# Gate logits of a hybrid encoder: pairs of tiles by seven block products, tanh through DRAM, gated sums on GpSimd

## Chip, cores, metric

The kernel runs on one core of a Trainium2 chip. The metric is the device time of one execution in microseconds (us), as the median of several runs. Engines are named as in the profile: PE (TensorE matmuls), PEld (its weight loads), DVE (VectorE), ACT (ScalarE), POOL (GpSimd), SP (SyncE, which here only issues DMAs).

## Reference

One layer of an encoder on x of 1024 positions by 1024 channels, in float32.

```python
h = rms_norm(x, g_mix[l])
z = h @ w_in[l]
u_fn, q, k, v, u_ssm, gate_logits = jnp.split(z, splits, axis=-1)
gates = jax.nn.sigmoid(gate_logits.reshape(b, s, N_BRANCH, D_MODEL))
y_fn = fourier_mix(u_fn) @ w_br_fn[l]
y_na = neighbourhood_attention(q * q_scale, k, v, na_rpb[l]) @ w_br_na[l]
y_ssm = ssm_branch(u_ssm, ...) @ w_br_ssm[l]
merged = gates[:, :, 0] * y_fn + gates[:, :, 1] * y_na + gates[:, :, 2] * y_ssm
x = x + merged @ w_out[l]
h = rms_norm(x, g_ffn[l])
x = x + jnp.square(jax.nn.relu(h @ w_up[l])) @ w_down[l]
```

The change concerns `gate_logits` (three times 1024 columns of `w_in`), the gates and the sum `merged`.

## The kernel before

All work is transposed: the normalised activations stand as `hT`, 1024 channels on 8 blocks of 128 partitions by 1024 positions in two halves of 512. Each float32 matmul is made of three on the fast float32 form: an operand is split in a high part (a cast on ACT) and a low part (a subtraction on DVE), and `three` multiplies high by high, high by low and low by high. So a weight tile of 128 output channels (128x1024, split as `wh` and `wl`) times `hT` for one half of the positions is 8 k-blocks x 3 = 24 matmuls of 128x512 (`proj`, line 171).

The middle of the kernel is a string of steps that sets the order in which work is written down. `q` steps make query and key, `t` steps (`logits`) make a tile of gate logits early and store its tanh in DRAM (`t_scr`), `fn` makes the Fourier input, `u` steps load a branch's rows from DRAM (`b_scr`, where they were spilled; the tiles are `act`), `at` finishes the attention, and `g` steps (`gate`) multiply a tile of a branch by its weight, form (tanh + 1) x product (line 1031, or 1029 for the first branch) and add it into the accumulator `mg` (line 1032). The first digit of `t` and `g` is the branch: 0 is the state space model (`ssm`), 1 the attention (`na`), 2 Fourier (`fn`); the second is the tile of 128 output channels, 0 to 7. In `gate`, tiles without an early `t` step make their logits in place: two halves of 24 matmuls. These are all 8 tiles of branch 0 and all 8 of branch 2. The last branch's sums are split into `mh` and `ml` (lines 199 and 200) for the output projection.

Three long computations (`ssm`, attention, Fourier) run as side generators: each third matmul of the main line calls `tick`, which lets a generator go on by its rate in steps. The order on each engine that results is fixed when the kernel is built; each engine works through its own list in order and waits at an instruction until its inputs and its buffers are there. SP's list of DMAs is such a list as well. Buffers come from pools: 36 slots of 4 KB per partition (`s`), 21 of 2 KB (`m`), 4 raw weights (`w`), 8 banks of PSUM.

Of the kernel before, what the change touches and what calls it, by code (L numbers as in the profile page):

```python
# [10 lines left out]
F32 = mybir.dt.float32  # L11
F32R = mybir.dt.float32r
I32 = mybir.dt.int32
AF = mybir.ActivationFunctionType
ALU = mybir.AluOpType

P = 128
# [3 lines left out]
H2 = 512  # L21
# [18 lines left out]
class Side:  # L40
    def __init__(self, gen, rate):
        self.gen = gen
        self.rate = rate
        self.credit = 0.0
        self.done = False
# [19 lines left out]
class Trunk:  # L65
# [806 lines left out]
    def queue(self):  # L872

        a = self.a
        wi = lambda i: (a["w_in"][i], [P, 8, P])
        q = [wi(14), wi(15)]
        q += [(a["w_v"][i], [P, 2, H2]) for i in range(4)]
        for step in self.steps:
            if step[0] == "q":
                q += [wi(2 + int(step[1])), wi(6 + int(step[1]))]  # L880
            elif step == "fn":
                q += [wi(0), wi(1)]
            elif step[0] in "tg":
                bi, d = int(step[1]), int(step[2])
                nm, br, kt, _ = self.order[bi]
                if step[0] == "t" or (bi, d) not in self.early:
                    q += [wi(16 + 8 * br + d)]
                if step[0] == "t":
                    self.early.add((bi, d))
                else:  # L890
                    q += [(a["w_br_" + nm][d], [P, kt, P])]
        q += [(a["w_out"][0, i], [P, 2, H2]) for i in range(4)]
        q += [(a["w_out"][1, i // 2][:, i % 2:i % 2 + 1, :], [P, 1, H2]) for i in range(8)]
        self.wq = q

    def run(self):
        nc, V, A, G = self.nc, self.nc.vector, self.nc.scalar, self.nc.gpsimd
        self.order = (("ssm", 2, 2, 0), ("na", 1, 4, 2), ("fn", 0, 2, 6))


        self.steps = ("t10 t11 q0 t12 q1 t13 t14 q2 t15 q3 t16 t17 fn u0 g00 g01 g02 at g03 g04 g05 g06 g07 u1 "
                      "g10 g11 g12 g13 g14 g15 u2 g16 g17 g20 g21 g22 g23 g24 g25 g26 g27").split()
        self.early = set()
        self.queue()
        self.zf, self.spilled = [], set()
# [15 lines left out]
        hT = []  # L921
# [4 lines left out]
        for half in range(2):  # L926
# [11 lines left out]
            for i in range(2):  # L938
                ps = self.proj(ws[i], hT, half)
# [9 lines left out]
        for t in range(8):  # L949
            half, c0 = t // 4, (t % 4) * P  # L950
            ps = self.ps([P, H2])
# [8 lines left out]
            r = 2 * (t % 2)  # L960
# [40 lines left out]
        acc = [None] * 8  # L1001
# [3 lines left out]
        def gate(bi, d):  # L1005
            nm, br, kt, ct = self.order[bi]
            act = acts[bi]
            early = (bi, d) in self.early
            if early:
                wb, = self.w_next(1, 1, 2)  # L1010
            else:
                wg, wb = self.w_next(2, 2, 2)
            if bi == 0:
                acc[d] = self.s([P, N], F32, "mg")
            for half in range(2):
                sl = slice(half * H2, half * H2 + H2)
                tg = self.m([P, H2], F32, "tg")
                if early:
                    self.dma(tg, self.t_scr[bi, d][:, sl])
                else:  # L1020
                    ps = self.proj(wg, hT, half)
                    A.activation(tg, ps, AF.Tanh, scale=0.5)  # L1022
                pb = self.ps([P, H2])
                pairs = []
                for k in range(kt):
                    pairs += self.three(wb[0][:, k, :], wb[1][:, k, :], *act[k][half])
                self.mm_main(pb, pairs)
                if bi == 0:
                    V.scalar_tensor_tensor(out=acc[d][:, sl], in0=tg, scalar=1.0, in1=pb, op0=ALU.add, op1=ALU.mult)
                    continue  # L1030
                V.scalar_tensor_tensor(out=tg, in0=tg, scalar=1.0, in1=pb, op0=ALU.add, op1=ALU.mult)
                V.tensor_tensor(out=acc[d][:, sl], in0=acc[d][:, sl], in1=tg, op=ALU.add)
                if bi == 2:
                    for q in (2 * half, 2 * half + 1):
                        if d % 4 == 0:
                            mg[q][d // 4] = (self.s([P, 4, 256], F32R, "mh"), self.s([P, 4, 256], F32R, "ml"))
                        hi, lo = mg[q][d // 4]
                        self.split(hi[:, d % 4, :], lo[:, d % 4, :], acc[d][:, 256 * q:256 * q + 256], 0.5)
            if bi == 2:
                acc[d] = None  # L1040

        def logits(bi, d):
            wg, = self.w_next(1, 1, 2)
            for half in range(2):
                ps = self.proj(wg, hT, half)
                tg = self.m([P, H2], F32, "tg")
                A.activation(tg, ps, AF.Tanh, scale=0.5)
                self.dma(self.t_scr[bi, d][:, half * H2:half * H2 + H2], tg)

        at, fft = None, None  # L1050
        need = (lambda: ssm, lambda: at, lambda: fft)

        def fetch(bi):
            need[bi]().finish()
            acts[bi] = self.unspill(self.order[bi][3], self.order[bi][2])

        for step in self.steps:
            if step[0] == "q":
                qk_in(int(step[1]))
                if at is None:  # L1060
                    at = self.side(attention(), 0.57)
            elif step == "fn":
                fn_in()
                fft = self.side(self.fft(), 0.5)
            elif step[0] == "u":
                fetch(int(step[1]))
            elif step == "at":
                at.finish()
            elif step[0] == "t":
                logits(int(step[1]), int(step[2]))  # L1070
            else:
                bi, d = int(step[1]), int(step[2])
                gate(bi, d)
                if d == 7:
                    acts.pop(bi)
# [5 lines left out]
        raw = [[None] * 8, [None] * 8]  # L1081
# [21 lines left out]
        for c in range(2):  # L1103
            wo = self.w_next(4 + 4 * c, 8 if c == 0 else 0, 8 if c == 0 else 1)
            cs = slice(c * H2, c * H2 + H2)
            for t in range(8):
                xr = self.m([P, H2], F32, "xr")
                self.dma(xr, self.a["x"][t * P:(t + 1) * P, cs])
                ps = self.ps([P, H2])
# [60 lines left out]
                t1[:] = []  # L1170

        ff.run()


class FeedForward:
# [8 lines left out]
    AHEAD_SUMS = 9  # L1184
    AHEAD_DOWN = 5
    RAW_DOWN = 9
    FIRST = 3
# [248 lines left out]
    def upto(self, name, steps, i, ahead, what):  # L1436
        at = self.done.get(name, 0)
        for s in steps[at:i + ahead + 1]:
            what(*s)
        self.done[name] = max(at, min(len(steps), i + ahead + 1))  # L1440

    def begin(self):

        n, first = self.PAIRS, range(self.FIRST)
        up = [(c, j) for j in (1, 2, 5, 6, 3, 7) for c in first]
        for c in range(self.FIRST, n):
            up.append((c, 1))
# [177 lines left out]
```

## Time and profile before

| what | value |
|---|---|
| time, median of 3 runs (lowest to highest) | 1411.34 us (1409.93 to 1414.94) |
| profiled execution, its own time | 1411.24 us |
| its span in the profile | 1409.5 us |
| mean granted clock of PE | 0.997 |
| PE busy, share of the span | 98% |
| DVE busy, share of the span | 67% |

The span is the time from the first to the last instruction in the profile; the rest of the profiled execution's time lies around it. An engine's busy time is the union of its instructions; matmuls overlap in it, so a matmul's own duration is longer than the distance from one start to the next.

### The profile page before, as it was taken

The page shows a single profiled execution, that of the slowest core. Times are in us where ns is not written, and L with a number is a line of the kernel's source. Part 1 is how long each engine was busy: PE and PEld are TensorE (multiplying, and loading weights), DVE is VectorE, ACT ScalarE, POOL GpSimd, SP SyncE. Part 2 cuts the span into 40 slices and gives each one's busy share as a digit, 9 for nine tenths or more (in the row PEclk, how much of TensorE's full clock was granted, in tenths as well). Part 3 has the DMA queues.
Part 4 walks back from the last instruction along what each step waited for, and adds up shares of the span by engine and source line. Part 5 has one row for each costly group of instructions (what it writes and reads, how often), then busy time and mean ns, then how long its engine had stood idle before and what let it go on. Part 6 is the DMA issues. An engine that isn't in the chain of part 4 may idle for free.

```text
span 1409.5 us, 18536 instructions
## 1 busy us (share of the span) xinstructions
PE 1376.9 (98%) x6520; PEld 1149.2 (82%) x6520; DVE 948.3 (67%) x1802; ACT 587.8 (42%) x1126; POOL 166.6 (12%) x345
## 2 busy tenths in 40 slices
PE   6999999999999999999999999999999999999997
PEld 5788878888888888888788788888888788888886
DVE  6778788768462314443516897777776899878767
ACT  5523454766552211122403664233333564444345
POOL 3800122312200000000000002121121100000000
PEclk9999999999999999999999999999999999999999
DMA  6352646665662219211334125444447885454303
GB/s 231 107 163 83 172 120 195 186 180 153 210 201 98 97 40 327 82 56 38 118 125 142 60 94 201 153 153 147 151 147 279 279 288 183 140 176 144 104 8 120
DMA packets 103437, 209.66 MB, mean 149 GB/s; under 512 B 18224, under 2 KB 34992, under 8 KB 103344
## 3 DMA queue, kind: packets, MB, share of 16 engines
q1 hardware_dynamic: 79872, 153.10, 33.3%
q0 software_dynamic: 23472, 55.38, 12.0%
q8 instruction: 51, 0.84, 0.3%
q14 instruction: 42, 0.34, 0.1%
HBM read 146.52 MB, written 56.62 MB: 144 GB/s over the span
## 4 chain that ended last, share of the span: by engine, by line
PE 90%; DVE 3%; POOL 2%; DMA 2%; ACT 1%; issue 1%; SPq 0%; DVEq 0%; POOLq 0%; ACTq 0%
PE ps L165 47%; PE ps L171 39%; PE ps L792 1%; PE ps L809 1%; PE ps L813 1%; DMA da<-h_scr 1%; DMA x<-in_x 0%; DMA wd<-in_w_down 0%; POOL pt L249 0%; POOL pt L250 0%; PE ps L1088 0%; PE ps L464 0%; ACT hTh L199 0%; POOL pt L282 0%; ACT wh L142 0%
## 5 line engine op out<-in xcount | busy, mean ns | idle before, releaser
L165 PE MATMUL ps<-dw,dh 128*128 128x512 f32 x1344 | 306.4, 390 | 2.2 <-DVE dw L197 1.9
L165 PE MATMUL ps<-fb,uw 128*128 128x512 f32 x1344 | 306.8, 390 | 1.4 <-DVE t L1147 1.0
L165 PEld LDWEIGHTS ps<-dw,dh 128*128 128x128 f32 x1344 | 252.2, 188 | 55.7 <-DVE dw L197 2.8
L165 PEld LDWEIGHTS ps<-fb,uw 128*128 128x128 f32 x1344 | 252.0, 188 | 54.4 <-PE ps L1088 1.2
L171 PE MATMUL ps<-hTh,wh 128*128 128x512 f32 x576 | 231.2, 402 | 3.0 <-ACT wh L142 1.6
L171 PE MATMUL ps<-hTl,wh 128*128 128x512 f32 x576 | 226.9, 394 | 1.1 <-DVE hTl L200 1.1
L171 PE MATMUL ps<-hTh,wl 128*128 128x512 f32 x576 | 226.9, 394 | 0.0
L171 PEld LDWEIGHTS ps<-hTh,wh 128*128 128x128 f32 x576 | 108.9, 189 | 24.0 <-ACT wh L142 2.4
L171 PEld LDWEIGHTS ps<-hTh,wl 128*128 128x128 f32 x576 | 108.8, 189 | 22.9 <-issue 0.2
L171 PEld LDWEIGHTS ps<-hTl,wh 128*128 128x128 f32 x576 | 109.0, 189 | 20.5 <-DVE hTl L200 1.5
L143 DVE TENSOR_TENSOR wl<-wr,wh 128x1024 fp32r<-128x1024 f32 (+2 forms) x76 | 70.8, 942 | 59.1 <-ACT wh L142 56.1
L196 ACT CAST dh<-da 128x512 fp32r<-128x512 f32 x112 | 69.4, 619 | 85.7 <-PE ps L165 61.3
L1384 DVE TENSOR_TENSOR x<-x,ps 128x512 f32<-128x512 f32 x112 | 74.1, 690 | 31.5 <-PE ps L165 31.5
L197 DVE TENSOR_TENSOR dh<-da,dh 128x512 fp32r<-128x512 f32 x112 | 78.0, 696 | 17.6 <-ACT dh L196 17.4
L1300 POOL DMA_DIRECT2D h_scr<-hx x48 | 26.0, 541 | 498.8 <-ACT hx L1270 396.2
L171 PE MATMUL ps<-act,wh 128*128 128x512 f32 x256 | 79.1, 390 | 0.0
L142 ACT CAST wh<-wr 128x1024 fp32r<-128x1024 f32 (+2 forms) x76 | 61.0, 822 | 37.2 <-PE ps L171 16.0
L196 ACT CAST uw<-us 128x512 fp32r<-128x512 f32 x64 | 38.1, 625 | 84.2 <-DVE us L1227 84.2
L1022 ACT ACTIVATE tg<-ps 128x512 f32<-128x512 f32 x32 | 19.1, 597 | 120.1 <-PE ps L171 114.1
L196 ACT CAST dw<-wd 128x512 fp32r<-128x512 f32 x80 | 49.4, 617 | 19.1 <-PE ps L165 18.4
L1272 DVE SCALAR_TENSOR_TENSOR hx<-hx 128x512 f32<-128x512 f32 x44 | 30.3, 689 | 40.0 <-ACT hx L1264 39.7
L197 DVE TENSOR_TENSOR dw<-wd,dw 128x512 fp32r<-128x512 f32 x80 | 55.6, 695 | 0.6 <-ACT dw L196 0.3
(288 smaller groups left out, 2097.4 us busy)
## 6 DMA issues: line engine op xcount, KB each, us to landing
da<-h_scr SPq DMA_DIRECT2D x112, 256.0 KB, 3.3
wr<-in_w_in SPq DMA_DIRECT2D x36, 512.0 KB, 4.6
wu<-in_w_up SPq DMA_DIRECT2D x32, 512.0 KB, 3.6
h_scr<-hs POOLq DMA_DIRECT2D x64, 256.0 KB, 2.6
wd<-in_w_down SPq DMA_DIRECT2D x64, 256.0 KB, 3.6
bm<-in_rpb POOLq DMA_DIRECT2D x64, 192.0 KB, 4.5
h_scr<-hx POOLq DMA_DIRECT2D x48, 256.0 KB, 2.5
vj<-v_scr POOLq DMA_DIRECT2D x32, 256.0 KB, 6.6
```

The lines of the kernel that those rows point to most:

```text
L142: self.nc.scalar.copy(hi, r)
L143: self.nc.vector.tensor_tensor(out=lo, in0=r, in1=hi.bitcast(F32), op=ALU.subtract)
L165: self.nc.tensor.matmul(out=out, lhsT=l, rhs=r, start=start and i == 0, stop=stop and i == last, skip_group_check=more)
L171: self.nc.tensor.matmul(out=out, lhsT=l, rhs=r, start=i == 0, stop=i == last)
L196: nc.scalar.copy(hi, src)
L197: nc.vector.tensor_tensor(out=lo, in0=src, in1=hi.bitcast(F32), op=ALU.subtract)
L792: nc.tensor.transpose(ps[:, i, :], sm[:, i * P:(i + 1) * P], self.ident)
L809: nc.tensor.matmul(out=ps, lhsT=v, rhs=two[i][x], start=i == 0 and x == 0, stop=False)
L1022: A.activation(tg, ps, AF.Tanh, scale=0.5)
L1272: V.scalar_tensor_tensor(out=x, in0=x, scalar=0.0, in1=x, op0=ALU.max, op1=ALU.mult)
L1300: self.nc.gpsimd.dma_start(out=self.t.h_scr[c, j - 1], in_=x)
L1384: self.nc.vector.tensor_tensor(out=self.x1[t][:, cs], in0=self.x1[t][:, cs], in1=self.banks[j][q], op=ALU.add)
```

## The change

Fourteen of the sixteen tiles that were projected in place are now made in seven pairs by a new class `Gates`; the first two tiles of branch 0 become early `t` steps (`t00`, `t01`). For a pair, the weights (two tiles by two halves of the channels) and `hT` (two halves of the channels by two halves of the positions) are seen as 2x2 blocks, and the four block products of each pair of rows and columns are made from seven products of sums of blocks instead of eight. A product has 4 k-blocks x 3 matmuls. The sums of blocks of `hT` are made once (`sums`, a side generator, 16 blocks `fg`), those of the weights for each pair (`sum_of`), and both are split (`prep`, `split`). All tanh tiles go to `t_scr`, those of the pairs by GpSimd's DMA queue, and `gate` only loads them, up to five halves ahead. The Fourier generator starts after the products (step `L`) and at twice the rate. The addition into `mg` moves to GpSimd.

```diff
-        self.steps = ("t10 t11 q0 t12 q1 t13 t14 q2 t15 q3 t16 t17 fn u0 g00 g01 g02 at g03 g04 g05 g06 g07 u1 "
-                      "g10 g11 g12 g13 g14 g15 u2 g16 g17 g20 g21 g22 g23 g24 g25 g26 g27").split()
+        self.steps = ("t10 t11 q0 t12 q1 t13 t14 q2 t15 q3 t16 t17 fn t00 at t01 L g00 g01 g02 g03 g04 g05 u1 g06 g07 "
+                      "g10 g11 g12 g13 u2 g14 g20 g21 g15 g22 g23 g16 g24 g25 g17 g26 g27").split()
+        self.pairs = [((bi, d), (bi, d + 1)) for bi in (0, 2) for d in range(0, 8, 2) if (bi, d) != (0, 0)]
...
-                tg = self.m([P, H2], F32, "tg")
-                if early:
-                    self.dma(tg, self.t_scr[bi, d][:, sl])
-                else:
-                    ps = self.proj(wg, hT, half)
-                    A.activation(tg, ps, AF.Tanh, scale=0.5)
+                while len(tgs) < 5 and ahead:
+                    self.dma(*ahead.pop(0)())
+                tg = tgs.pop(0)
...
-                V.tensor_tensor(out=acc[d][:, sl], in0=acc[d][:, sl], in1=tg, op=ALU.add)
+                G.tensor_tensor(out=acc[d][:, sl], in0=acc[d][:, sl], in1=tg, op=ALU.add)
...
-                fft = self.side(self.fft(), 0.5)
+            elif step == "L":
+                gates.run()
+                del gates
+                fft = self.side(self.fft(), 1.0)
...
                 at.finish()
+                gates = Gates(self, hT, lambda: fetch(0))
+                gates.begin()
+                sums = self.side(gates.sums(), 1.0)
...
+    AHEAD = 2
+    AHEAD_SUMS = 4
+    FIRST = 2
...
+    def sums(self):
...
+        def put(j, k, src):
...
+            t = self.t.s([P, 2, H2], F32R, "fg")
+            self.f[j].append(t)
+            self.t.split(t[:, 0], t[:, 1], src)
+
+        for k in range(4):
+            (ah, al), (bh, bl) = self.block(1, 1, k), self.block(1, 2, k)
+            tt(raw[k], fl(bh), fl(ah), S)
+            tt(raw[k], raw[k], fl(al), S)
+            tt(raw[k], raw[k], fl(bl), A)
+            put(5, k, raw[k])
+            yield
+            yield
+        for k in range(4):
+            h, l = self.block(2, 2, k)
+            tt(raw[k], fl(h), raw[k], S)
+            tt(raw[k], raw[k], fl(l), A)
+            put(6, k, raw[k])
...
+    def sum_of(self, c, j):
...
+        x, y, op = {5: lambda: (a(2, 1), a(2, 2), ALU.add), 6: lambda: (u[c, 5], a(1, 1), ALU.subtract),
+                    3: lambda: (a(1, 2), u[c, 6], ALU.subtract), 7: lambda: (a(1, 1), a(2, 1), ALU.subtract)}[j]()
+        u[c, j] = self.t.m([P, H2], F32, "us")
+        self.nc.vector.tensor_tensor(out=u[c, j], in0=x, in1=y, op=op)
...
+    def product(self, c, j):
...
+        for k in range(4):
+            f, ks = self.operand(j, k), slice(k * P, k * P + P)
+            t.mm(ps, t.three(w[:, 0, ks], w[:, 1, ks], *f), start=first and k == 0, stop=k == 3, more=not first)
+            t.tick()
+        if j in (1, 5, 6):
+            o = t.m([P, H2], F32, "k")
+            A.copy(o, ps)
+            self.keep[c, j] = o
+            return
+        x = t.m([P, H2], F32, "gx")
+        if j == 4:
+            A.activation(x, ps, AF.Tanh, scale=0.5)
+        else:
+            V.tensor_tensor(out=x, in0=ps, in1=self.keep.pop((c, {2: 1, 3: 6, 7: 5}[j])), op=ALU.add)
+            A.activation(x, x, AF.Tanh, scale=0.5)
...
+        self.nc.gpsimd.dma_start(out=t.t_scr[bi, d][:, half * H2:half * H2 + H2], in_=x)
...
+        self.order = [(c, j) for j in (1, 2, 5, 6, 3, 7, 4) for c in first]
```

How this moves instructions, at three places. In the rows below a number behind a name is that of a write, so equal numbers are the same tile as it was written at one point.

DVE before, at the attention's last low part (`spl`), which is followed by the Fourier steps' low parts (`vl`) and the first gated tile:

```order
L197 TENSOR_TENSOR spl_4524<-OT_3813,sph_4523 128x1024
L197 TENSOR_TENSOR vl_4506<-ps_4507,vh_4505 128x512
L197 TENSOR_TENSOR vl_4506<-ps_4537,vh_4505 128x512
L1029 SCALAR_TENSOR_TENSOR mg_4464<-tg_4465,ps_4545 128x512
L707 TENSOR_TENSOR yf_4486<-ps_4563,bs_4609 128x256
L708 COPY yf_4486<-ps_4563 128x1
L709 TENSOR_TENSOR yf_4486<-ps_4563,bs_4609 128x255
```

DVE in the changed kernel behind the same low part, where the sums of blocks of `hT` begin (`tr`, line 1212; `hTh` and `hTl` are the high and low parts):

```order
L197 TENSOR_TENSOR spl_4471<-OT_3813,sph_4470 128x1024
L1212 TENSOR_TENSOR tr_4525<-hTh_345,hTh_163 128x512
L1212 TENSOR_TENSOR tr_4526<-hTh_345,hTh_163 128x512
L1212 TENSOR_TENSOR tr_4527<-hTh_347,hTh_165 128x512
L1212 TENSOR_TENSOR tr_4528<-hTh_347,hTh_165 128x512
L1212 TENSOR_TENSOR tr_4525<-tr_4525,hTl_164 128x512
```

Fifty-nine rows after `spl` DVE reaches the low part of the first weight sum that product 5 multiplies (`uw_4701`, made of `us_4625`), between other sums and low parts of blocks (`fg`); `tr_4525` to `tr_4528` and `tq` are the sums themselves:

```order
L1279 TENSOR_TENSOR us_4767<-wu_4513,us_4699 128x512
L1212 TENSOR_TENSOR tq_4742<-tq_4742,hTl_170 128x512
L1212 TENSOR_TENSOR tq_4754<-tq_4754,hTl_170 128x512
L197 TENSOR_TENSOR fg_4678<-tq_4674,fg_4678 128x512
L197 TENSOR_TENSOR fg_4691<-tq_4687,fg_4691 128x512
L197 TENSOR_TENSOR uw_4701<-us_4625,uw_4701 128x512
L197 TENSOR_TENSOR fg_4711<-tq_4708,fg_4711 128x512
L197 TENSOR_TENSOR fg_4723<-tq_4720,fg_4723 128x512
L197 TENSOR_TENSOR uw_4735<-us_4665,uw_4735 128x512
```

So the low part that product 5 needs comes 64 rows behind `spl`; the first low part of any weight (that of product 1) comes 35 rows behind it, among the sums. On ACT, the casts of the blocks stand behind the tanh of t00 and t01 (`tg`, line 1044; the third one is the first half of t01):

```order
L196 CAST sph_4470<-OT_3813 128x1024
L1044 ACTIVATE tg_4482<-ps_4436 128x512
L1044 ACTIVATE tg_4510<-ps_4485 128x512
L1044 ACTIVATE tg_4574<-ps_4521 128x512
L196 CAST fg_4532<-tr_4525 128x512
L196 CAST fg_4544<-tr_4526 128x512
```

The cast of the first block thus comes behind the tanh of t01's first half. On SP's queue, the loads of the attention's rows (`act`, 128x1024) stood before behind branch weights:

```order
L111 DMA wr_5441<-in_w_br_na 128x512
L111 DMA wr_5481<-in_w_br_na 128x512
L111 DMA wr_5521<-in_w_br_na 128x512
L111 DMA act_5389<-b_scr 128x1024
L111 DMA act_5390<-b_scr 128x1024
```

In the changed kernel they stand behind two loads of tanh (`tg`) and a branch weight, in the stretch of the Fourier steps:

```order
L111 DMA wr_6156<-in_w_br_na 128x512
L111 DMA tg_5981<-t_scr 128x512
L111 DMA tg_6000<-t_scr 128x512
L111 DMA wr_6212<-in_w_br_na 128x512
L111 DMA act_6036<-b_scr 128x1024
L111 DMA act_6037<-b_scr 128x1024
L111 DMA act_6040<-b_scr 128x1024
```

They have moved behind loads that wait for slots of tiles which that stretch still reads.

## Rows read from the trace of the kernel before

**Rows 1.** The page: the span, the first part (busy time, share of the span and number of instructions of each engine), the granted clock by slices in tenths of full speed, and the chain of work that ended last by engine.
```profile
span 1409.5 us, 18536 instructions
PE 1376.9 (98%) x6520; PEld 1149.2 (82%) x6520; DVE 948.3 (67%) x1802; ACT 587.8 (42%) x1126; POOL 166.6 (12%) x345
PEclk9999999999999999999999999999999999999999
...
PE 90%; DVE 3%; POOL 2%; DMA 2%; ACT 1%; issue 1%; SPq 0%; DVEq 0%; POOLq 0%; ACTq 0%
```

**Rows 2.** Busy time by windows of the stage that the change rewrites. Columns: from and to in us, length, then for PE, PEld, DVE, ACT and POOL the busy us and the instructions that began, the granted clock as a share, the share of the DMA engines, GB/s. The first row is from another answer of the same view.
```profile
490.00:525.00 35.00, 35.00 (x157) 28.97 (x156) 6.83 (x10) 6.45 (x12) 0.00 (x0) 1.00 0.09 30
...
450.00:480.00 30.00, 30.00 (x164) 26.03 (x163) 10.81 (x16) 8.28 (x13) 0.00 (x0) 1.00 0.27 91
...
527.00:550.00 23.00, 23.00 (x103) 19.04 (x102) 3.89 (x7) 3.26 (x6) 0.00 (x0) 1.00 0.95 357
550.00:600.00 50.00, 50.00 (x222) 41.42 (x221) 30.75 (x48) 8.90 (x15) 0.00 (x0) 1.00 0.40 129
600.00:630.00 30.00, 30.00 (x134) 24.85 (x133) 13.05 (x23) 8.38 (x17) 0.00 (x0) 1.00 0.22 66
630.00:665.00 35.00, 34.35 (x152) 28.17 (x151) 13.04 (x25) 8.44 (x19) 0.00 (x0) 1.00 0.07 20
665.00:700.00 35.00, 34.05 (x151) 27.86 (x150) 19.70 (x31) 14.39 (x25) 0.00 (x0) 1.00 0.33 103
```

**Rows 3.** Waits of PE from 600 to 810 us: who waited for whom, us in total, times, the longest.
```profile
PE ps L171 <- ACT wh L142: 1.6, 2, 1.0
```

**Rows 4.** Timeline of PE: start, us, engine, line, operation, out<-in, tiles. Six matmuls of a gate projection and the start of a seventh, then the end of the first half of the first gate tile (g00, which the change makes as t00) and the Fourier steps' half-width matmuls behind it.
```profile
491.44 0.39 PE L171 MATMUL ps<-hTh,wh 128*128 128x512 f32 x1
491.67 0.39 PE L171 MATMUL ps<-hTl,wh 128*128 128x512 f32 x1
491.89 0.39 PE L171 MATMUL ps<-hTh,wl 128*128 128x512 f32 x1
...
492.57 0.39 PE L171 MATMUL ps<-hTh,wl 128*128 128x512 f32 x1
492.80 0.39 PE L171 MATMUL ps<-hTh,wh 128*128 128x512 f32 x1
...
415.27 0.39 PE L171 MATMUL ps<-hTh,wl 128*128 128x512 f32 x1
415.50 0.40 PE L165 MATMUL ps<-ct,fh 128*128 128x256 f32 x2
...
416.81 0.28 PE L165 MATMUL ps<-ct,fl 128*128 128x256 f32 x1
416.93 0.63 PE L171 MATMUL ps<-act,wh 128*128 128x512 f32 x2
```

**Rows 5.** Timeline of DVE where it has a queue of operations of 128x512.
```profile
1136.58 0.70 DVE L197 TENSOR_TENSOR dh<-da,dh 128x512 fp32r<-128x512 f32 x1
1137.18 0.70 DVE L197 TENSOR_TENSOR dw<-wd,dw 128x512 fp32r<-128x512 f32 x1
1137.78 0.70 DVE L197 TENSOR_TENSOR dh<-da,dh 128x512 fp32r<-128x512 f32 x1
1138.38 0.70 DVE L197 TENSOR_TENSOR dw<-wd,dw 128x512 fp32r<-128x512 f32 x1
```

**Rows 6.** Groups of ACT and DVE from the page and from 416 to 700 us by shape: count | busy us, mean ns of one | idle time before them, and what ended it.
```profile
L196 ACT CAST uw<-us 128x512 fp32r<-128x512 f32 x64 | 38.1, 625 | 84.2 <-DVE us L1227 84.2
L1022 ACT ACTIVATE tg<-ps 128x512 f32<-128x512 f32 x32 | 19.1, 597 | 120.1 <-PE ps L171 114.1 <-issue 6.0
```

**Rows 7.** Timeline of DVE at the attention's last low part, and a window behind it (columns as in rows 2).
```profile
415.67 1.23 DVE L197 TENSOR_TENSOR spl<-OT,sph 128x1024 fp32r<-128x1024 f32 x1 [1.11 <-ACT sph L196]
...
416.90:442.70 25.80, 25.80 (x152) 22.74 (x151) 7.33 (x13) 5.04 (x10) 2.15 (x4) 1.00 0.38 131
```

**Rows 8.** Timeline of SP's queue (issues) when the attention's rows are loaded, and the DMA part for 520 to 560 us: the busy tenths of the DMA engines in 40 slices, and issues with KB each and median us to landing.
```profile
527.04 4.19 SPq L111 DMA_DIRECT2D act<-b_scr  x8
531.57 4.27 SPq L111 DMA_DIRECT2D tg<-t_scr  x4
...
DMA  0000005599998999999999999999700759978779
...
act<-b_scr SPq DMA_DIRECT2D x8, 512.0 KB, 7.3
tg<-t_scr SPq DMA_DIRECT2D x12, 256.0 KB, 6.0
```

**Rows 9.** Groups of POOL by shape, whole span, columns as in rows 6.
```profile
L1300 POOL DMA_DIRECT2D h_scr<-hs x64 | 34.6, 540 | 116.4 <-DVE hs L1296 108.4 <-issue 8.0
...
L241 POOL TENSOR_TENSOR bbar<-tb 128x256 f32<-128x256 f32 x1 | 1.1, 1067 | 0.1
L244 POOL TENSOR_TENSOR bbar<-tb 128x256 f32<-128x256 f32 x1 | 0.9, 887 | 0.1
...
L242 POOL TENSOR_TENSOR tb<-ssb,pt 128x256 f32<-128x256 f32 x1 | 0.7, 652 | 0.1
L239 POOL TENSOR_TENSOR tb<-ssb,pt 128x256 f32<-128x256 f32 x1 | 0.6, 622 | 0.0
...
L239 POOL TENSOR_TENSOR pt<-pt 128x16 f32<-128x16 f32 x2 | 0.4, 221 | 0.1
```

**Rows 10.** Groups of DVE from 416 to 700 us by shape, columns as in rows 6.
```profile
L1032 DVE TENSOR_TENSOR mg<-mg,tg 128x512 f32<-128x512 f32 x32 | 21.9, 691 | 0.8
L1031 DVE SCALAR_TENSOR_TENSOR tg<-tg,ps 128x512 f32<-128x512 f32 x32 | 21.9, 686 | 48.0 <-PE ps L171 39.6 <-ACT tg L1022 8.3
```

More of the change, by code (lines that the diff above doesn't have):

```diff
@@ L882, in queue @@
                 q += [wi(0), wi(1)]
+            elif step == "L":
+                self.early.update(x for p in self.pairs for x in p)
             elif step[0] in "tg":
@@ L1007, in gate @@
             act = acts[bi]
-            early = (bi, d) in self.early
-            if early:
-                wb, = self.w_next(1, 1, 2)
-            else:
-                wg, wb = self.w_next(2, 2, 2)
+            wb, = self.w_next(1, 1, 2)
             if bi == 0:
@@ L1016, in gate @@
                 sl = slice(half * H2, half * H2 + H2)
-                tg = self.m([P, H2], F32, "tg")
-                if early:
-                    self.dma(tg, self.t_scr[bi, d][:, sl])
-                else:
-                    ps = self.proj(wg, hT, half)
-                    A.activation(tg, ps, AF.Tanh, scale=0.5)
+                while len(tgs) < 5 and ahead:
+                    self.dma(*ahead.pop(0)())
+                tg = tgs.pop(0)
                 pb = self.ps([P, H2])
@@ L1042, in logits @@
         def logits(bi, d):
-            wg, = self.w_next(1, 1, 2)
+            wg, = self.w_next(1, *((1, 2) if bi else (1 - d, 1 - d)))
             for half in range(2):
@@ L1048, in logits, with tanh_of @@
                 self.dma(self.t_scr[bi, d][:, half * H2:half * H2 + H2], tg)
+        tgs = []
+        def tanh_of(bi, d, half):
+            tgs.append(self.m([P, H2], F32, "tg"))
+            return tgs[-1], self.t_scr[bi, d][:, half * H2:half * H2 + H2]
+        ahead = [lambda b=int(x[1]), d=int(x[2]), h=h: tanh_of(b, d, h) for x in self.steps if x[0] == "g" for h in range(2)]
         at, fft = None, None
@@ L1063, in run @@
                 fn_in()
-                fft = self.side(self.fft(), 0.5)
+            elif step == "L":
+                gates.run()
+                del gates
+                fft = self.side(self.fft(), 1.0)
             elif step[0] == "u":
```

106 lines of the change are left out of this document (added).

## Prediction

> **What bounds the kernel now.** I read the page first: PE is busy for 98% of the span, DVE for 67%, ACT for 42%, POOL for 12%, and 90% of the chain that ended last is PE [rows 1]. The granted clock is full in every slice, which is the 2.4 GHz level, so a matmul that goes away is worth its full-speed time and no more. Then I cut the stretch that the change rewrites, from about 415 us to 700 us, into windows: PE is busy for 35.00 of 35 us and 50.00 of 50 us, and only the last two windows miss 0.65 and 0.95 us [rows 2]. The waits of PE there add up to 1.6 us, twice for a weight's high part [rows 3]. So this stage is a dense stream of matmuls. Removing matmuls shortens it one for one, and every wait that the change puts in front of PE lengthens it one for one, because no slack is left to swallow it.
>
> **What is removed.** Two gate tiles had 2 tiles x 2 halves x 8 k-blocks x 3 matmuls = 96 matmuls; seven products have 7 x 4 x 3 = 84. Seven pairs save 7 x 12 = 84. A matmul of 128x512 shows 0.39 us, but the next one starts 0.2267 us after it: six of them from 491.44 to 492.80 us take 1.36 us [rows 4]. The pitch counts, so the saving is 84 x 0.2267 = **19.0 us**.
>
> **What is added, steady part.** Each pair now costs DVE four weight sums, seven low parts and three sums with a kept product, 14 operations of 128x512. DVE shows 0.70 us for one, but starts one every 0.60 us when they queue up [rows 5]; 14 x 0.60 = 8.4 us. ACT has seven casts, three copies and four tanh, 14 x about 0.60 to 0.62 [rows 6] = 8.5 us. A pair's matmuls take 84 x 0.2267 = 19.0 us, so both engines lie under PE by more than half. I cost the steady part at nothing; its cover is those 10 us of slack per pair.
>
> **What is added, at the start.** This is where I put the loss. The products 5, 6, 7 and 4 need 16 sums and differences of blocks of the transposed activations, four k-blocks for each. Products 5 and 7 take three operations and a low part for a block, 6 and 4 two and a low part: 4 x (4 + 3 + 4 + 3) = 56 DVE operations of 128x512, or 33.6 us at 0.60. In the order they stand directly behind the attention's last low part, and 52 of them come ahead of the low part that product 5 waits for, with 12 operations of the first weights between them. Before, DVE was nearly free there: it is busy for 7.33 of 25.8 us from 416.9 us on [rows 7].
> The working, on the clock of the trace of before, in which the order of PE is unchanged up to 415.5 us (the end of the first half of tile t00) [rows 4]:
> - PE then has 72 matmuls of t00 and t01, to 415.5 + 72 x 0.2267 = 431.8 us, then products 1 and 2 of two pairs, 48 matmuls or 10.9 us, to 442.7 us if nothing is late.
> - DVE is free at 415.67 + 1.23 = 416.9 us [rows 7]. Twelve sums end at 424.1 us. The thirteenth operation is a low part, which needs ACT's cast, and ACT has the tanh of t01's first half ahead of that cast. That half ends on PE at 415.5 + 48 x 0.2267 = 426.4 us; tanh 0.60 and cast 0.62 [rows 6] make it 427.6 us.
> - From there to the low part of product 5's first weight block, stand 52 operations (64 in all from the first sum on): 52 x 0.60 = 31.2 us, so it is ready at 458.8 us. The first weight block of all has its low part 23 operations after 427.6, at 441.4 us, so products 1 and 2 wait some 8 to 10 us for it, run until about 452 us, and are not what is late last.
> - PE starts product 5 at 458.8 instead of 442.7 us: **16.1 us lost**. Behind it DVE delivers a low part every 0.6 to 2 us against products of 2.7 us, so it isn't late again, but the 16.1 us don't come back.
> Bounds: without the wait for ACT, 64 operations from 416.9 us end at 455.3, a loss of 12.6 us; with 0.70 us for each operation, as if they did not overlap, the chain ends at 427.6 + 36.4 = 464.0, a loss of 21.3 us. I take 16.1, because long queues of such operations in the trace do run at 0.60 [rows 5].
>
> **What moves behind the gates.** The Fourier steps and the first branch tiles now stand together behind the products. PE has there 96 x 0.2267 + 144 x 0.12 us (the pitch of the half-width matmuls, twelve of which run from 415.50 to 416.93 us [rows 4]), about 39 us. Before, gate projections stood between Fourier steps and covered their round trips over ACT, DVE and DRAM. The eight loads of the attention's rows (512 KB each) are issued behind two tanh loads and a branch weight on SP's in-order queue, and these wait for slots that are freed some 25 us into this stretch. Before, eight such loads were issued in 4.19 us and took 7.3 us each to land, with the DMA engines 95% busy [rows 2, 8], so these 4 MB take about 4.2 + 7.3 = 11.5 us, and with tanh tiles beside them up to 15. They land 36 to 40 us into the stretch and PE wants the first at 39 us: 0 to 4 us, and I take 1. The stores of tanh by GpSimd, 28 x 0.54 us [rows 9], lie on an engine with no work there (0.00 us busy in each window from 450 us on [rows 2]); a tile's load follows its store by tens of microseconds, since tiles are stored in pairs and read much later. I cost them at nothing; without this cover each would cost one landing, 6.0 us for tanh tiles [rows 8].
>
> **Sums on GpSimd.** The 32 additions cost DVE 21.9 us [rows 10], which DVE had to spare: its saving is worth nothing to PE. On POOL no addition of this size is in the trace. The rows nearest are 128x256 with two full operands, 0.89 and 1.07 us; with one operand broadcast they take 0.62 to 0.66, and 128x16 takes 0.22 [rows 9]. Doubled, and with the small one's 0.22 taken off once, that gives 1.02 (from 0.62) to 1.91 us (from 1.07); DVE's own 0.69 is the lower end. I take 1.55, from the 0.89 us row, which has the same kind of operands and the shorter time. In the mixed part one tile of the attention's branch (24 matmuls) and two of the Fourier branch (12 each) take PE 10.9 us and POOL 6 x 1.55 = 9.3 us, so POOL keeps up; the point from which it doesn't is 10.9 / 6 = 1.8 us. At the end of the stage a sum comes 0.9 us later than DVE's, ahead of the cast and the low part that the output projection needs. I take 1 us for this, between 0 and 4.
>
> GPSIMD Engine Reference of the Trainium skill, section 3.1, speaks against this edit: elementwise work takes GpSimd about 2.6 cycles per element at 1.2 GHz, some twice VectorE's time. By that page an addition would be 512 x 2.6 / 1.2 = 1.1 us, an estimate, and the sum would be the same within 0.5 us. No row of this trace has the operation at that size.
>
> **The sum.** 1411.2 (the profiled execution; span 1409.5 and 1.7 around it; the median of the runs is 1411.3) - 19.0 + 16.1 + 1 + 1 = 1410.3, say **1410 us**: no change that can be told. About 0.3%, or 4.2 us, is what a measurement of this kernel can tell from no change.
>
> **Rivals.**
> - *The start is cheaper.* DVE's queue is what I cost most exactly, but ACT's wait and the pitch carry 3.5 us of it, and if the later stage loses nothing the time is 1411.2 - 19.0 + 12.6 = 1404.8. If the sums found a place under the attention's end, which the order denies, as they stand behind its last low part, the whole 19 us would show: 1392. The first is quite possible, the second hardly. Together 1392 to 1407: 0.32.
> - *GpSimd becomes the bound of the branch stage.* If an addition takes 2.13 us (twice the 1.07 us row) POOL needs 12.8 us for each 10.9 us of PE, 1.9 us lost in each of four groups, 7.6 us, and the last sum comes 1.4 us later. With the rest of the sum, 1410.3 - 1 + 9 = 1418: slower. It decides from 1.8 us on. For it: the two full-operand rows. Against it: the 0.62 us rows. An addition that has to wait for one DVE operation in front of it would come to the same price, 1.55 + 0.70 = 2.25 us by rows 5 and 9. Together 0.15. (SBUF — State Buffer of the Trainium skill, section "Who interferes with whom", states such a wait: GpSimd's reads and VectorE's operations with two SBUF inputs shut each other out for a whole instruction. No row here has both at once.)
> - *The loads of the attention's rows starve PE.* If they land one transfer later than worked out, PE waits 7.3 us [rows 8] behind the Fourier steps with nothing else in its order: 1410.3 - 1 + 7.3 = 1416.6. Against it: the weights and tanh tiles ahead of them are small. 0.10.
> - *My forecast*, 1407 to 1415.5: 0.43.
>
> **How the numbers follow.** Faster by over 0.3% (under 1407): 0.32. Within 0.3%: 0.43. Slower (over 1415.6): 0.25. The range is 1399 to 1420. Below, it holds the cheap start of 1404.8 and reaches about halfway to 1392, for an order of events at the start that I misread; above, it holds both slow rivals and the upper bound of the start (21.3 us instead of 16.1 makes 1415.5) with 4.5 us behind it. The forecast's own range is 1405 to 1415.
>
> **What would show it.** PE: about 84 fewer matmuls of 128x512, and between the end of t01 and product 5 gaps of 12 to 21 us in all, some 8 to 10 of it ahead of products 1 and 2 and the rest ahead of product 5, put down to DVE's low parts and ACT's casts. DVE: some 40 us without a pause from about 417 us, at 0.60 from start to start. In the later products PE without gaps. Behind them at most 4 us of gaps, for a load of the attention's rows. POOL: additions of 1.0 to 1.9 us. I am wrong if PE's gap at the start is under 10 us; if the matmuls' pitch rises in the products; or if additions on POOL take over 1.8 us and PE's gaps are found in the branch stage.

## Result and profile after

The changed kernel takes 1429.09 us (median; 1427.82 to 1432.41) against 1412.11 us of the kernel before in the same comparison: ratio 1.0122, 95% interval 1.0107 to 1.0137. It is 17 us slower, where 1410 us, no change, was forecast, and lies above the range.

The page of the changed kernel, as in [rows 1]:

```profile
span 1428.1 us, 18836 instructions
PE 1369.1 (96%) x6436; PEld 1138.8 (80%) x6436; DVE 1020.3 (71%) x1910; ACT 623.4 (44%) x1198; POOL 228.2 (16%) x405
PEclk9999999999998999899999999999999999999999
```

PE has 84 matmuls fewer (6436 for 6520), as expected. Its busy time fell only from 1376.9 to 1369.1 us, 7.8 us instead of 19, and the clock shows two slices under nine tenths. Its idle time rose from 1409.5 - 1376.9 = 32.6 us to 1428.1 - 1369.1 = 59.0 us. So the 18.6 us of span are + 26.4 us of gaps and - 7.8 us of busy time: the saving of 19.0 us is there, less some 11 us in which matmuls ran at the lower clock.

The windows of the stage (columns as in [rows 2]) say where:

```profile
432.00:445.00 13.00, 6.20 (x18) 4.17 (x17) 13.00 (x23) 6.32 (x11) 0.00 (x0) 0.74 0.05 20
445.00:460.00 15.00, 9.95 (x40) 7.09 (x38) 14.97 (x26) 6.63 (x13) 1.10 (x2) 0.92 0.05 19
460.00:480.00 20.00, 19.99 (x79) 16.35 (x80) 11.51 (x18) 8.01 (x15) 1.03 (x2) 0.89 0.30 95
480.00:500.00 20.00, 20.00 (x90) 16.58 (x89) 9.24 (x14) 8.46 (x15) 2.75 (x6) 1.00 0.42 142
...
580.00:600.00 20.00, 13.75 (x58) 11.43 (x57) 4.90 (x8) 3.10 (x6) 4.54 (x8) 0.74 0.98 342
...
680.00:700.00 20.00, 18.54 (x81) 14.69 (x80) 18.48 (x27) 9.06 (x22) 13.42 (x10) 1.00 0.69 225
700.00:720.00 20.00, 14.06 (x53) 10.54 (x53) 20.00 (x27) 9.68 (x19) 10.76 (x6) 0.93 0.47 142
```

Three places have gaps: 432 to 460 us (the start of the products), 580 to 600 us (the start of the Fourier steps) and 680 to 720 us (the end of the branch stage). Between them PE is as dense as before. In or behind each place the granted clock is lower: 0.74, 0.92 and 0.89 at the first, 0.74 at the second, 0.93 at the third. The waits of PE from 400 to 720 us (columns as in [rows 3]) give each gap a name:

```profile
PE ps L165 <- ACT uw L196: 11.5, 3, 6.7
PE ps L165 <- DMA ct<-in_dft_c: 6.2, 1, 6.2
PE ps L171 <- DVE wl L143: 2.7, 4, 0.9
PE ps L171 <- ACT mh L199: 2.6, 1, 2.6
PE ps L171 <- DVE ml L200: 2.3, 1, 2.3
```

**The start.** PE's timeline: the first product's matmul follows a gap of 6.74 us, then the first of product 5 (`fg`) follow 3.97 and 0.83 us.

```profile
439.45 0.80 PE L165 MATMUL ps<-hTh,uw 128*128 128x512 f32 x1 [6.74 <-ACT uw L196]
440.47 0.63 PE L165 MATMUL ps<-hTh,uw 128*128 128x512 f32 x1
440.90 0.63 PE L165 MATMUL ps<-hTl,uw 128*128 128x512 f32 x1
...
444.45 0.39 PE L165 MATMUL ps<-hTl,uw 128*128 128x512 f32 x1
444.68 0.62 PE L165 MATMUL ps<-hTh,uw 128*128 128x512 f32 x2
...
456.97 0.73 PE L165 MATMUL ps<-fg,uw 128*128 128x512 f32 x2 [3.97 <-ACT uw L196]
458.53 1.22 PE L165 MATMUL ps<-fg,uw 128*128 128x512 f32 x2 [0.83 <-ACT uw L196]
```

From 440.47 us on the matmuls follow each other at 0.43 us, and from 444.45 on at 0.23 us: the first ones behind the gap ran at the lower of the two levels (1.2 GHz), those from about 444 us on at 2.4 GHz. DVE's timeline in the same stretch (start, us; the last column is how often):

```profile
416.88 2.49 DVE L1212 TENSOR_TENSOR tr<-hTh,hTh 128x512 f32<-128x512 f32 x4
...
428.45 1.90 DVE L197 TENSOR_TENSOR fg<-tr,fg 128x512 fp32r<-128x512 f32 x3 [4.27 <-ACT fg L196]
...
441.71 0.68 DVE L197 TENSOR_TENSOR uw<-wu,uw 128x512 fp32r<-128x512 f32 x1
...
459.27 0.68 DVE L197 TENSOR_TENSOR uw<-us,uw 128x512 fp32r<-128x512 f32 x1
```

The sums begin at 416.88 us behind the attention's last low part, wait 4.27 us for ACT's cast behind the tanh of t01, and go on without a pause, one every 0.60 us. Product 1's low part starts at 441.71 and product 5's at 459.27 us. The gap of 6.74 us ended when ACT cast product 1's weight (`uw`), and that cast was held by DVE's queue as well: on ACT it stands behind a cast of a block (`fg`) that waited for its sum (`tr`) from DVE.

```profile
438.26 0.62 ACT L196 CAST fg<-tr 128x512 fp32r<-128x512 f32 x1 [0.64 <-DVE tr L1212]
438.79 1.66 ACT L196 CAST uw<-wu 128x512 fp32r<-128x512 f32 x3
```

**The Fourier table.** GpSimd's queue (issues, in order):

```profile
581.85 0.55 POOL L1321 DMA_DIRECT2D t_scr<-gx  x1 [4.84 <-issue]
582.94 0.54 POOL L1321 DMA_DIRECT2D t_scr<-gx  x1 [0.53 <-ACT gx L1316]
586.25 0.54 POOL L1321 DMA_DIRECT2D t_scr<-gx  x1 [2.78 <-ACT wh L142]
586.78 0.75 POOL L667 DMA_DIRECT2D ct<-in_dft_c  x1
```

The load of `ct` is behind the stores of the last tanh tiles. The last of these could go only at 586.25 us, when the last product had passed through ACT (its tanh ran there from 585.36 to 585.96 us); `ct` was issued at 586.78 and PE started on it at 591.51 us, after 6.25 us of nothing.

**The branch stage.** Groups of DVE and POOL from 640 to 725 us by shape (columns as in [rows 6]):

```profile
L1028 DVE SCALAR_TENSOR_TENSOR tg<-tg,ps 128x512 f32<-128x512 f32 x32 | 21.1, 679 | 18.5 <-PE ps L171 18.5
L200 DVE SCALAR_TENSOR_TENSOR ml<-mg,mh 128x256 fp32r<-128x256 f32 x32 | 20.3, 671 | 0.0
L143 DVE TENSOR_TENSOR wl<-wr,wh 128x512 fp32r<-128x512 f32 x11 | 10.3, 939 | 0.0
L143 DVE TENSOR_TENSOR wl<-wr,wh 128x256 fp32r<-128x256 f32 x8 | 9.2, 1160 | 1.5 <-POOL mg L1029 1.5
```

```profile
L1029 POOL TENSOR_TENSOR mg<-mg,tg 128x512 f32<-128x512 f32 x32 | 45.9, 1452 | 81.1 <-DVE tg L1028 81.1
```

An addition on POOL took 1.45 us. DVE's low parts got longer beside it: `ml` of 128x256 took 671 ns (423 ns in the same stage of before), `wl` of 128x256 1160 ns (424 ns before) and `wl` of 128x512 939 ns (689 ns before). Line 1028 did not get longer (679 ns; 686 ns in [rows 10]): it has one operand in PSUM. One case in DVE's timeline and then in POOL's:

```profile
697.83 0.42 DVE L200 SCALAR_TENSOR_TENSOR ml<-mg,mh 128x256 fp32r<-128x256 f32 x1
698.16 1.51 DVE L143 TENSOR_TENSOR wl<-wr,wh 128x256 fp32r<-128x256 f32 x1
```

```profile
698.05 1.35 POOL L1029 TENSOR_TENSOR mg<-mg,tg 128x512 f32<-128x512 f32 x1 [1.03 <-DVE tg L1028]
```

The first low part, at 697.83 us, took 0.42 us. POOL's addition began at 698.05 us and lasted 1.35 us; the low part of the same size that begins right after it on DVE, at 698.16 us, took 1.51 us. It goes the other way too: two additions that began just behind a `wl` of 128x1024 on DVE, at 702.16 and 706.80 us, took 2.21 us each, where the shortest took 1.27.

### The profile page after: what moved, and what is told of

The parts are those of the page before. It is cut to its first block, busy times and chain, and to the rows that moved or that the text cites. A ratio compares the mean times of both kernels' runs of the same rounds, so it can differ in the third digit from the quotient of the medians.

```text
span 1428.1 us, 18836 instructions
## 1 busy us (share of the span) xinstructions
PE 1369.1 (96%) x6436; PEld 1138.8 (80%) x6436; DVE 1020.3 (71%) x1910; ACT 623.4 (44%) x1198; POOL 228.2 (16%) x405
## 4 chain that ended last, share of the span: by engine, by line
PE 89%; DVE 5%; DMA 2%; issue 2%; ACT 1%; POOL 1%; SPq 0%; DVEq 0%; POOLq 0%; ACTq 0%
PE ps L165 55%; PE ps L171 30%; PE ps L792 1%; PE ps L809 1%; PE ps L813 1%; DVE wl L143 1%; DMA x<-in_x 1%; DMA da<-h_scr 1%; DMA wd<-in_w_down 1%; DVE tq L1212 0%; PE ps L1099 0%; DVE tr L1212 0%; DMA ct<-in_dft_c 0%; DVE fg L197 0%; DVE ml L200 0%
## 5 line engine op out<-in xcount | busy, mean ns | idle before, releaser
L171 PE MATMUL ps<-hTh,wh 128*128 128x512 f32 x352 | 143.6, 409 | 1.6 <-DVE hTl L200 1.6
L171 PE MATMUL ps<-hTl,wh 128*128 128x512 f32 x352 | 139.9, 398 | 1.9 <-DVE hTl L200 1.9
L171 PE MATMUL ps<-hTh,wl 128*128 128x512 f32 x352 | 140.0, 398 | 0.0
L165 PE MATMUL ps<-fg,uw 128*128 128x512 f32 x336 | 81.9, 399 | 5.1 <-ACT uw L196 4.8
L197 DVE TENSOR_TENSOR uw<-us,uw 128x512 fp32r<-128x512 f32 x92 | 60.8, 686 | 34.7 <-ACT uw L196 34.5
L165 PEld LDWEIGHTS ps<-fg,uw 128*128 128x128 f32 x336 | 64.6, 193 | 20.1 <-ACT uw L196 5.7
L171 PEld LDWEIGHTS ps<-hTh,wl 128*128 128x128 f32 x352 | 66.9, 190 | 14.2 <-issue 0.2
L171 PEld LDWEIGHTS ps<-hTh,wh 128*128 128x128 f32 x352 | 67.1, 191 | 13.5 <-DVE hTl L200 2.1
L171 PEld LDWEIGHTS ps<-hTl,wh 128*128 128x128 f32 x352 | 67.0, 190 | 13.2 <-DVE hTl L200 2.3
L165 PE MATMUL ps<-hTh,uw 128*128 128x512 f32 x168 | 54.8, 399 | 6.8 <-ACT uw L196 6.7
```

The costliest lines, as they stand in the source:

```text
L165: self.nc.tensor.matmul(out=out, lhsT=l, rhs=r, start=start and i == 0, stop=stop and i == last, skip_group_check=more)
L171: self.nc.tensor.matmul(out=out, lhsT=l, rhs=r, start=i == 0, stop=i == last)
L197: nc.vector.tensor_tensor(out=lo, in0=src, in1=hi.bitcast(F32), op=ALU.subtract)
```

## Experiments

Each is compared with the kernel before (1412 us). The theory after the traces: three separate losses, the sums at the start, `ct` behind the stores, and GpSimd's additions that hold up DVE, each with a stretch at the lower clock behind its gaps. The rivals were that a loss would come back at the next place, or that the branch stage was late for another reason.

**Sums back on DVE.**

```diff
-                G.tensor_tensor(out=acc[d][:, sl], in0=acc[d][:, sl], in1=tg, op=ALU.add)
+                V.tensor_tensor(out=acc[d][:, sl], in0=acc[d][:, sl], in1=tg, op=ALU.add)
```

> The changed kernel with the 32 gated sums put back on DVE, nothing else. Theory (POOL's additions shut out DVE's operations with two SBUF operands, and DVE is the engine that is late at the stage's end): the stage from 640 to 725 us loses its 7.7 us of PE gaps down to about 1.6, and the stretch at the lower clock behind them goes too; wl 128x256 goes back from 1.16 to about 0.43 us and ml from 0.67 to 0.42; time 1420 to 1424 us against 1429. Rival (the output projection's weights land late, by DMA, and DVE only looks late): DVE's operations are short again but the gaps stay; 1427 to 1430.

Measured: 1417.95 us, ratio 1.0049 (1.0030 to 1.0067), 11.1 us faster than the changed kernel and more than expected. PE's waits from 400 to 730 us, and DVE's low parts:

```profile
PE ps L165 <- ACT uw L196: 11.5, 3, 6.7
PE ps L165 <- DMA ct<-in_dft_c: 6.3, 1, 6.3
```

```profile
L200 DVE SCALAR_TENSOR_TENSOR ml<-mg,mh 128x256 fp32r<-128x256 f32 x32 | 12.5, 415 | 0.0
L143 DVE TENSOR_TENSOR wl<-wr,wh 128x512 fp32r<-128x512 f32 x11 | 7.3, 683 | 1.3 <-ACT wh L142 1.3
L143 DVE TENSOR_TENSOR wl<-wr,wh 128x256 fp32r<-128x256 f32 x8 | 3.2, 416 | 0.0
```

No gap is left in the branch stage, not even the two (1.6 us) that the kernel before had there [rows 3], and the low parts have their old lengths. The rival of late weights falls.

**A useless addition on GpSimd.**

```diff
-                G.tensor_tensor(out=acc[d][:, sl], in0=acc[d][:, sl], in1=tg, op=ALU.add)
+                V.tensor_tensor(out=acc[d][:, sl], in0=acc[d][:, sl], in1=tg, op=ALU.add)
+                if "d" not in dump:
+                    dump["d"] = self.m([P, H2], F32, "dump")
+                G.tensor_tensor(out=dump["d"], in0=tg, in1=tg, op=ALU.add)
...
```

> The changed kernel with the gated sums on DVE, as in the first run, and beside each of them an addition of the same size on GpSimd whose result nobody reads (tanh tile plus itself, into one scratch tile). It tells apart two ways in which the additions on GpSimd cost time. Theory (they shut DVE out while they read): wl and ml of 128x256 on DVE are long again (means over 0.6 us) and gaps come back at the stage's end: 1421 to 1429 us. Rival (the sum itself comes later, 1.45 us in place of 0.69, in the chain to mh and ml): as the first run, 1416 to 1419 us.

Measured: 1427.65 us, ratio 1.0111 (1.0092 to 1.0129). The result of these additions goes nowhere, and yet 9.7 of the 11.1 us are back (1.0 us of longer wait for `ct` among them). DVE's groups from 640 to 725 us and PE's waits for it:

```profile
L1029 DVE TENSOR_TENSOR mg<-mg,tg 128x512 f32<-128x512 f32 x30 | 27.0, 899 | 0.2
L1028 DVE SCALAR_TENSOR_TENSOR tg<-tg,ps 128x512 f32<-128x512 f32 x32 | 21.4, 677 | 10.0 <-PE ps L171 10.0
L200 DVE SCALAR_TENSOR_TENSOR ml<-mg,mh 128x256 fp32r<-128x256 f32 x24 | 13.6, 589 | 0.0
L143 DVE TENSOR_TENSOR wl<-wr,wh 128x256 fp32r<-128x256 f32 x8 | 4.9, 613 | 0.9 <-POOL dump L1032 0.9
```

```profile
PE ps L171 <- DVE wl L143: 7.5, 6, 2.4
```

DVE's operations with two operands in SBUF are long again (line 1029, the gated sum, 899 ns instead of 683; `ml` 589, `wl` 613 ns), the one with an operand in PSUM is not (677 ns). So being shut out is enough to cost what the additions cost, on a DVE that here does the 32 sums as well. Which share of the 11.1 us in the changed kernel came from the later sum isn't separated; PE's waits there also name `mh` (2.6 us), which stands behind POOL's sum.

**The kernel before with its sums on GpSimd.**

```diff
-                V.tensor_tensor(out=acc[d][:, sl], in0=acc[d][:, sl], in1=tg, op=ALU.add)
+                G.tensor_tensor(out=acc[d][:, sl], in0=acc[d][:, sl], in1=tg, op=ALU.add)
```

> The kernel before with its 32 gated sums on GpSimd, nothing else. Theory (port shared by GpSimd and DVE, wherever the additions stand): additions of 1.3 to 1.5 us, DVE's wl and ml of 128x256 with means over 0.5 us in the branch stage, but DVE has more slack there than in the changed kernel because gate projections stand between: 2 to 4 us slower, nearly all at the last tile. Rival 1 (in any order DVE is late as in the changed kernel): 6 to 8 us slower. Rival 2 (the additions slow DVE only in the changed order): the same within 1 us, wl and ml unchanged.

Measured: 1411.91 us, ratio 1.0008 (0.9995 to 1.0020): no change. The theory's 2 to 4 us and the first rival's 6 to 8 us are missed; the second rival had the time right, but not that `wl` of 128x512 would be as before. DVE's groups from 530 to 705 us:

```profile
L200 DVE SCALAR_TENSOR_TENSOR ml<-mg,mh 128x256 fp32r<-128x256 f32 x32 | 12.2, 421 | 30.6 <-ACT mh L199 30.6
L143 DVE TENSOR_TENSOR wl<-wr,wh 128x512 fp32r<-128x512 f32 x14 | 11.5, 852 | 7.4 <-ACT wh L142 7.4
```

`wl` of 128x512 is longer there too (852 for 689 ns), `ml` isn't. Additions and low parts seldom meet when gate projections stand between the tiles: the low parts take some 2 us more than before in all (11.5 us for the fourteen `wl` of 128x512, 9.3 before), against 16.8 us more in the changed kernel than with the sums on DVE (20.3 + 10.3 + 9.2 against 12.5 + 7.3 + 3.2). PE's waits are those of the kernel before (1.6 us). The same edit costs nothing in the order of before and 11 us in the order of the change.

**The Fourier table earlier.**

```diff
+    def ct_in(self):
+        self.ct = self.m([P, 2, 256], F32R, "ct")
+        self.nc.gpsimd.dma_start(out=self.ct, in_=self.a["dft_c"].rearrange("i p x -> p i x"))
...
-        ct = self.m([P, 2, 256], F32R, "ct")
-        G.dma_start(out=ct, in_=self.a["dft_c"].rearrange("i p x -> p i x"))
+        ct = self.ct
...
                 self.last()
+                self.t.ct_in()
```

> The changed kernel with the load of the Fourier table ct issued ahead of the last products' tanh stores on GpSimd's queue. Theory (the table is late only because it is queued behind stores that wait for the last tanh): the 6.25 us gap at 585 us goes, with the lower clock behind it (about 3 us): 1419 to 1422 us. Rival (the Fourier stage's large tables pt, 512 KB each, or the first branch's rows are late next, since DMA is 98% busy there): the gap stays as a wait for pt or act, 1426 to 1429.

Measured: 1421.86 us, ratio 1.0076 (1.0057 to 1.0095), 7.2 us faster than the changed kernel. The gap at 585 us is gone; one of 0.9 us for a branch weight's cast has come in its place, and the waits of the branch stage are 8.0 us. So the table was late by its queue.

```profile
PE ps L171 <- ACT wh L142: 0.9, 1, 0.9
```

**No sums at the start.** The generator `sums` is empty and `operand` returns plain blocks:

```diff
-        if j < 4:
-            return self.block(*{1: (1, 1), 2: (2, 1), 3: (2, 2)}[j], k)
-        t = self.f[j][k]
-        return t[:, 0], t[:, 1]
+        return self.block(*{1: (1, 1), 2: (2, 1), 3: (2, 2), 5: (1, 2), 6: (2, 2), 7: (1, 2), 4: (2, 1)}[j], k)
...
```

> The changed kernel without the sums of blocks of the activations: products 5, 6, 7 and 4 multiply plain blocks instead, so the gates of the fourteen paired tiles are not the reference's. The 56 DVE operations and 16 ACT casts at the start are gone. Theory (DVE's queue at the start is what PE waits for): the gaps between 432 and 460 us (11.8 us) shrink to under 2 us and the lower clock behind them (about 5 us) goes too; 1411 to 1414 us. Rival (the first weights of the products are late by themselves, their loads or splits): a gap of over 5 us stays at 432 us; over 1418.

Measured: 1409.16 us, ratio 0.9982 (0.9971 to 0.9993), 19.9 us faster than the changed kernel and 2 us less than expected. The window from 432 to 460 us has PE busy all the time and at full clock:

```profile
432.00:460.00 28.00, 28.00 (x125) 23.20 (x124) 14.22 (x22) 12.38 (x22) 1.10 (x2) 1.00 0.30 103
```

The first Fourier matmul, less its wait for `ct`, is due at 574.13 - 5.33 = 568.8 us here and at 591.51 - 6.25 = 585.3 us in the changed kernel. These are 16.5 us apart. This execution was already late by 1.4 us before the experiment's edit acts (`spl` starts at 417.18 us here, at 415.74 in the changed kernel), so the start cost 17.9 us: 11.8 us of gaps and the rest at the lower clock. Behind the Fourier matmul the spans (21.7 us apart) hold another 0.9 us for the shorter wait for `ct` and some 4 us, of which a shorter gap for `ml` (0.9 for 2.3 us) is the only one named.

**The sums at half the rate.**

```diff
-                sums = self.side(gates.sums(), 1.0)
+                sums = self.side(gates.sums(), 0.5)
```

> The changed kernel with the sums generator at half the rate, so that on DVE the low part of product 5's first weight stands 32 rows behind the attention's last low part instead of 64 and that of product 1 stands 23 rows behind instead of 35; the same operations, another order. Theory (the start's loss is the length of DVE's queue ahead of the first products): product 1's low part is ready at about 438 us instead of 445, product 5 doesn't wait any more; about 6 us of gap instead of 11.8 and a shorter stretch at the lower clock: 1418 to 1422 us. Rival (the 56 sums are work that DVE has to do before PE can go on, in any order): the gap moves behind products 1 and 2 or to product 7, 1426 to 1430.

Measured: 1416.04 us, ratio 1.0026 (1.0015 to 1.0037), 13 us faster than the changed kernel, and 2 us better than expected. PE's waits:

```profile
PE ps L165 <- DMA ct<-in_dft_c: 7.6, 1, 7.6
PE ps L165 <- ACT uw L196: 2.8, 2, 2.2
```

The wait for weights at the start fell from 11.5 to 2.8 us (in the branch stage the gap for `ml` is shorter as well, 0.8 for 2.3 us; why stays open). The same 56 operations cost little when they don't stand ahead of the first products' low parts. The rival (the work itself is the loss) falls.

**All three.** The edits of the first, the `ct` and the rate experiments, and the first three weight blocks split ahead of the sums:

```diff
                 gates.begin()
-                sums = self.side(gates.sums(), 1.0)
+                gates.first()
+                sums = self.side(gates.sums(), 0.5)
...
+    def first(self):
+        self.upto("prep", 0, 2, self.prep)
```

> The changed kernel with all three causes taken away at once: gated sums on DVE; the table ct issued ahead of the last stores; the sums generator at half the rate, and the first three weight blocks split ahead of the sums. If the three losses are separate and complete, what is left is the 84 matmuls saved: 1411.3 - 19.0 - 1.6 (the two gaps of the kernel before, which the run with DVE's sums does not have) = 1391, 1390 to 1396 us. Rival (a loss taken away at one place comes back at the next, since DMA is 98% busy in the Fourier stretch and DVE has 20.00 of 20 us in the branch stage): 1400 or more.

Measured: 1395.54 us, ratio 0.9884 (0.9866 to 0.9903), 16 us faster than the kernel before and 33.5 us faster than the change, in the expected range and 4.5 us above its sum. PE's busy time, and its waits from 400 to 730 us:

```profile
PE 1357.7 (97%) x6436; PEld 1130.7 (81%) x6436; DVE 1021.2 (73%) x1942; ACT 621.9 (45%) x1198; POOL 182.0 (13%) x373
```

```profile
PE ps L165 <- ACT uw L196: 1.3, 1, 1.3
PE ps L171 <- ACT wh L142: 0.9, 1, 0.9
PE ps L165 <- DVE fg L197: 0.5, 1, 0.5
```

PE's busy time is 1376.9 - 1357.7 = 19.2 us less than before, which is the 84 matmuls at 0.2267 us (19.0) to within 0.2 us. The mean granted clock is 0.999 (0.986 in the changed kernel). The difference of 1369.1 - 1357.7 = 11.4 us, with the same 6436 matmuls, is what the lower clock cost in the changed kernel, but for about 1 us by estimate: each of the eight more gaps also leaves the end of one matmul (0.39 - 0.23 us) in the busy time. The losses were separate: the gains of the three runs add up to 11.1 + 7.2 + 13.0 = 31.3 us, and together, with the early splits, they gave 33.5. Matmuls at the same place in PE's order show where: against this run, the changed kernel is late by 1.3 us at 416 us of its own time, 15.4 us at 566, 23.6 us at 631 and 34.7 us at 785. So the start cost 14.2, the Fourier steps 8.1 and the branch stage 11.1 us more than here; of the start's 17.9 us, 3.7 are still in this run, 1.8 of them as the two waits for `uw` and `fg`, and with the 0.9 us for `wh` they are what keeps it above 1391 us.

## Why the prediction was wrong

- *The saving, 19.0 us*: right; 19.2 us in the last experiment.
- *The start, 16.1 us*: right in place and chain, near in size (17.9 us by the run without sums). Product 5's low part was forecast to be ready at 458.8 us and ran from 459.27 to 459.95; product 1's was forecast for 441.4 and ran from 441.71 to 442.39. DVE's pitch (0.60 us), ACT's wait (until 427.6 us forecast, until 428.45 in the timeline) and the gaps' places were as worked out. The gaps themselves are 11.8 us, just under the forecast's 12 to 21, and 6.74 instead of 8 to 10 ahead of product 1, since PE began it with the weight's high part, at 439.45 us. The other 6 us or so are matmuls between and behind the gaps at half the clock, of which the forecast said nothing; that the total came out within 2 us is in part luck. A rise of the pitch in the products was one of its signs of being wrong, and it came (0.43 us from 440 to 444 us).
- *The steady part, nothing*: right. From 480 to 580 us PE is busy in every window.
- *The stores by GpSimd, nothing*: wrong. The step looked at POOL's busy time and not at what is queued behind the stores. The loads of the Fourier tables go by the same in-order queue, and in the new order `ct` stood behind three stores that wait for the last tanh. This cost 7.2 us by the medians and 8.1 us in the profiled executions (6.25 us of gap and the matmuls behind it at half the clock, a granted clock of 0.50 in the window from 589 to 595 us). The step followed the order on SP's queue and left out POOL's.
- *The loads of the attention's rows, 1 us (rival 7.3)*: 0. They were issued in time and no wait names them.
- *The sums on GpSimd, 1 us*: wrong by 10 us. The mean duration was in the forecast bounds (1.45 us, 1.55 taken) and under the point of 1.8 us, so POOL kept up. What decided was DVE's time rather than POOL's (the share of the later sums is not separated): the text costed DVE's relief at nothing because DVE had time to spare, and did not ask what DVE does in the new stage. In 680 to 720 us DVE is busy for 18.48 and 20.00 of 20 us, since the branch tiles now stand without gate projections between them; every 0.2 to 0.7 us by which a low part gets longer can go to PE. The rival named the shutting out, and priced it only as longer additions (2.25 us; two of 32 took 2.21) and not as longer operations on DVE; its time, 1418, was too low as well, because it had 9 us for the additions instead of 11.1 and neither the wait for `ct` nor the lower clock in it.
- *What was not in the sum at all*: the stretches at half the clock behind the longer gaps; about 11 us over the whole execution, contained in the three losses.

In numbers: 1411.3 - 19.0 - 1.6 (the gaps of before, which the run with DVE's sums shows gone) + 17.9 + 9.0 + 11.1 = 1428.7; measured 1429.1. The Fourier steps stand in it with 9.0 us: in the traces the changed kernel loses 8.1 us there against the run with the earlier table, which itself waits 0.9 us. The last 0.4 us are less than runs of one kernel differ by (1427.8 to 1432.4).

SBUF — State Buffer of the Trainium skill, section "Who interferes with whom", says that a DVE instruction with two SBUF inputs and a GpSimd instruction that reads SBUF shut each other out for a whole instruction. The run with the useless additions agrees: 899 for 683 ns with two SBUF inputs, 677 ns with one in PSUM.

GPSIMD Engine Reference of the Trainium skill, section 3.1, gives 2.6 cycles per element at 1.2 GHz, from which 1.1 us was estimated; the additions took 1.45 us on average in the changed kernel and 1.38 in the kernel before with the same edit, and 1.27 at the shortest, so longer than by that page.

## What to carry to other kernels

When an engine that looks idle gets a new instruction, read what else stands in its in-order list, its DMA issues above all: here a store that waited for a late result held the load behind it. An offload from DVE to GpSimd is priced by what DVE then does beside it, in the new order, and not by GpSimd's duration: with slack on DVE it cost nothing, without it 11 us. A queue of preparation that is short in total can still stop PE if all of it stands ahead of the first product; half the rate of its generator gave back 13 us without one operation less.

## What the runs showed of the hardware

- A gap of 6 to 7 us on PE was followed by matmuls at half the clock: 0.43 us instead of 0.23 us between starts, from 440 to 444 us after 6.74 us of nothing. Over this execution the lower clock cost about 11 us, beside 26.4 us more of gaps than before. It was not only the longest gaps: two of 2.65 and 2.35 us, at 709 and 715 us, were followed by matmuls 0.43 us apart from 717.5 to 720 us.
- DVE operations of 128x256 with both operands in SBUF took up to 1.5 us instead of 0.42 us when a GpSimd addition of 128x512 had begun just before them; an addition that began just behind a DVE operation of that kind took up to 2.21 us instead of 1.27 in the changed kernel.
